# Attention: key transposes from word copies, inside the next key-value block

## The chip, the cores and the metric

The kernel runs on one core of one Trainium2 chip. The metric is the device time of one execution in microseconds, taken as the median of several runs. TensorE (PE) multiplies and transposes, VectorE (DVE), ScalarE (ACT) and GpSimd (POOL) do elementwise work, SyncE (SP) issues the loads of the weights. PEld is TensorE's loading of the stationary operand. POOL can issue DMAs too, on a queue of its own.

## The reference

A trunk of two layers over 256 tokens with a residual width of 2048: a multi-head latent attention, then a Mamba-2 mixer, each followed by a squared-ReLU MLP. All is fp32. The change is in the attention, which has 16 heads and runs once:

```python
q = (rms_norm(c_q, q_norm_g) @ w_uq).reshape(B, S, MLA_HEADS, QK_HEAD_DIM)
kv = (rms_norm(c_kv, kv_norm_g) @ w_ukv).reshape(B, S, MLA_HEADS, QK_NOPE_DIM + V_HEAD_DIM)
k_nope, v = jnp.split(kv, [QK_NOPE_DIM], axis=-1)
k = jnp.concatenate([k_nope, k_rope], axis=-1)       # k_rope: one for all heads
q, k = rms_norm(q, qn_g), rms_norm(k, kn_g)
# rotary embedding of the last 64 of 192 columns of q and k
s = jnp.einsum('bqhd,bkhd->bhqk', q_blk, k) * scale
p = jax.nn.softmax(jnp.where(mask, s, -jnp.inf), axis=-1)
o = jnp.einsum('bhqk,bkhd->bqhd', p, v)
```

## The kernel before

Tokens lie on partitions, in two tiles of 128. Matrix products take each weight as a sum of two parts that TensorE multiplies in a fast rounded format (float32r): ScalarE rounds the loaded weight (`wh`, L102), VectorE computes the rest (`wl`, L103). The main products of a block are L339 and L340 (with `wh`) and L343 (with `wl`).

The attention works in eight **units** of two heads. What has to be multiplied along the head dimension is transposed on TensorE, as a product with the identity; L937 does it on tiles held as float32r, L939 and L985 on fp32 tiles. For the transposes of a **word copy** a DMA that POOL issues copies an fp32 tile, bit by bit, into a tile declared float32r; the queries of units 1 to 7 have such a copy (`qw`, L897).

The loop at L1018 has one **pass** for each u from 0 to 7. Different units are in different steps at a time. In pass u, TensorE's order (which is the order in which the code is written; the order on the other engines is set by a scheduler at build time) is:

- `s0q(u + 1)`: the query block of unit u + 1, two weight units of 384 columns; in pass 7 a block of the output projection (`wob`) stands here.
- `s1(u - 1, "k")`: the six 128x128 transposes of the keys of unit u - 1, the **key group**. Four go into one PSUM bank and two into the next. ScalarE evacuates the first bank (L948), VectorE the second (L946), which holds the rope columns of both heads.
- `s0kv(u)`: the key-value block of unit u, two weight units of 512 columns. Between its two **halves** stands `s3(u - 2)`: the six transposes of the probabilities of unit u - 2 (L985), evacuated by VectorE (L987) and ScalarE (L989). After the block ScalarE takes sums of squares (L296) and POOL computes a root (L289, L290).
- `s2(u - 1)`: the scores of unit u - 1 (L961 and L962, per head), then the softmax on VectorE and ScalarE; its last step is a scaling on VectorE (L975).
- `s4(u - 2)`: probabilities times values (L997, L998).
- `s1(u, "q")`: the six transposes of the queries, the **query group**. With a word copy five come from it (L937) and the last one from the fp32 tile (L939).

Beside these, `k_norm(u)` writes the normalized keys `kn` (VectorE L916, ScalarE L918), `q_norm` the queries (L887), and `q_rope` rotates the queries on POOL (L798 to L801) and issues their word copy. After the loop the keys of unit 7 are transposed, and the last scores and outputs are computed between blocks of the output projection.

The line in `s1` that chooses between the two kinds of transposes takes a word copy wherever one exists, for keys as for queries:

```python
src, words = U[u][name + "n"], U[u].get(name + "w")
...
if words is not None and (i, t) != (1, 1):
```

Of the kernel before, what the change touches and what calls it, by code (L numbers as in the profile page):

```python
# [20 lines left out]
F32 = mybir.dt.float32  # L21
F32R = mybir.dt.float32r
# [6 lines left out]
P = 128  # L29
# [6 lines left out]
HD = 192  # L36
# [178 lines left out]
class Trunk:  # L215
# [610 lines left out]
    def mla_body(self, mp, gain):  # L826
        nc, d = self.nc, self.d
# [39 lines left out]
        U = [dict() for _ in range(UNITS)]  # L867

        def s0q(u, accs=None, mid=None):
            U[u]["q"] = self.block([("uq", u)], cqT, n=384, accs=accs, mid=mid)  # L870

        def q_stats(u):
            accs = U[u]["q"]
            ssq = self.stat(4)
            for t in range(2):
                for h in range(2):
                    self.square_sum(accs[t][:, h * HD:(h + 1) * HD], ssq[:, 2 * t + h:2 * t + h + 1], HD ** -0.5)
            U[u]["qr"] = self.root(ssq, eps4, 4)

        def q_norm(u):  # L880
            accs, r = U[u]["q"], U[u]["qr"]
            qn = mp.tile([P, 2, 2 * HD], F32, tag="qn", name=f"qn{u}", bufs=2)
            for t in range(2):
                for h in range(2):
                    rc = r[:, 2 * t + h:2 * t + h + 1]
                    for o, i, n in ((h * P, 0, P), (256 + h * 64, P, 64)):
                        nc.vector.scalar_tensor_tensor(qn[:, t, o:o + n], accs[t][:, h * HD + i:h * HD + i + n], rc,  # L887
                                                       gq[:, i:i + n], ALU.mult, ALU.mult)
            U[u]["qn"] = qn

        def q_rope(u, ins=None):
            qn = U[u]["qn"]
            with self.tc.issue_after(ins) if ins else nullcontext():
                self.rope(mp, qn[:, :, 256:384].rearrange("p t (h f) -> p t h f", h=2))
                if u:
                    U[u]["qw"] = mp.tile([P, 2, 2 * HD], F32R, tag="qw", name=f"qw{u}", bufs=2)
                    nc.gpsimd.dma_start(U[u]["qw"].bitcast(F32), qn)  # L897

        def s0kv(u, mid=None):
            accs = self.block([("ukv", u)], ckvT, mid=mid)  # L900
            v = mp.tile([P, 2, 2, P], F32, tag="v", name=f"v{u}", bufs=3)
            ssq = self.stat(4)
            for t in range(2):
                for h in range(2):
                    self.square_sum(accs[t][:, h * P:(h + 1) * P], ssq[:, 2 * t + h:2 * t + h + 1], HD ** -0.5)
            for t in range(2):
                nc.scalar.activation(v[:, t].rearrange("p h f -> p (h f)"), accs[t][:, 256:512], AF.Copy)
            U[u]["kv"], U[u]["kr"], U[u]["v"] = accs, self.root(ssq, krss, 4), v

        def k_norm(u):  # L910
            accs, r = U[u]["kv"], U[u]["kr"]
            kn = mp.tile([P, 2, 2 * HD], F32, tag="kn", name=f"kn{u}", bufs=2)
            for t in range(2):
                for h in range(2):
                    rc = r[:, 2 * t + h:2 * t + h + 1]
                    nc.vector.scalar_tensor_tensor(kn[:, t, h * P:(h + 1) * P], accs[t][:, h * P:(h + 1) * P], rc, gk[:, 0:P],  # L916
                                                   ALU.mult, ALU.mult)
                    nc.scalar.activation(kn[:, t, 256 + h * 64:320 + h * 64], kro[:, t], AF.Copy, scale=rc)  # L918
            U[u]["kn"] = kn

        def s1(u, name):


            src, words = U[u][name + "n"], U[u].get(name + "w")
            dst = self.ktile(self.xtp, F32)
            if name == "q":
                nc.gpsimd.memset(dst[64:128, 2], 0.0)
                nc.gpsimd.memset(dst[0:64, 3], 0.0)
            for i in range(2):
                b = self.bank()  # L930
                parts = 2 - i
                for j in range(parts):
                    for t in range(2):
                        o = j * 256 + t * P
                        k = (2 * i + j) * P
                        if words is not None and (i, t) != (1, 1):
                            nc.tensor.transpose(b.bitcast(F32R)[:, o:o + P], words[:, t, k:k + P], self.ident_r)  # L937
                        else:
                            nc.tensor.transpose(b[:, o:o + P], src[:, t, k:k + P], self.ident)  # L939
                v = b[:, :parts * 256].rearrange("p (k n) -> p k n", k=parts)  # L940
                if i and name == "q":
                    for h in range(2):
                        r = slice(64 * h, 64 * h + 64)
                        nc.scalar.activation(dst[r, 2 + h], b[r, 0:256], AF.Copy)
                elif (i == 0) == (name == "q"):
                    nc.vector.tensor_copy(dst[:, 2 * i:2 * i + parts], v)  # L946
                else:
                    nc.scalar.activation(dst[:, 2 * i:2 * i + parts], v, AF.Copy)  # L948
            U[u][name + "T"] = dst
# [29 lines left out]
        def s3(u):  # L979
            p = U[u]["p"]  # L980
            pT = self.ktile(self.xtp, F32).rearrange("p a b -> p (a b)")
            for h in range(2):
                b = self.bank()
                for i in range(3):
                    nc.tensor.transpose(b[:, i * P:(i + 1) * P], p[:, h * 384 + i * P:h * 384 + (i + 1) * P], self.ident)  # L985
                if h == 0:
                    nc.vector.tensor_copy(pT[:, 0:384], b[:, 0:384])  # L987
                else:
                    nc.scalar.activation(pT[:, 384:768], b[:, 0:384], AF.Copy)  # L989
            U[u]["pT"] = pT  # L990

        def s4(u):
            pT, v = U[u]["pT"], U[u]["v"]
            b = self.bank()
            for h in range(2):
                o = h * 256
                nc.tensor.matmul(b[:, o:o + 256], v[:, 0, h], pT[:, h * 384:h * 384 + 256], start=True, stop=False)  # L997
                nc.tensor.matmul(b[:, o + P:o + 256], v[:, 1, h], pT[:, h * 384 + 256:h * 384 + 384], start=False, stop=True)  # L998
            h, lo = oT[u // 2]
            k = (u % 2) * 2  # L1000
            self.split_out(h[:, k:k + 2], lo[:, k:k + 2], b.rearrange("p (k n) -> p k n", k=2))
            U[u].clear()
# [4 lines left out]
        def wob(nb, q, accs=None):  # L1007
            return self.block(wo(nb, [q]), self.from_tiles(oT, 4 * q), accs=accs, first=q == 0, last=q == 3)
# [9 lines left out]
        for u in range(UNITS):  # L1018
            if 0 < u and u + 1 < UNITS:
                s0q(u + 1)  # L1020
                q_stats(u + 1)
            if u == UNITS - 1:
                a0 = wob(0, 0)
            if u >= 1:
                s1(u - 1, "k")
            if 0 < u and u + 1 < UNITS:
                q_norm(u + 1)
            s0kv(u, (lambda: s3(u - 2)) if u >= 2 else None)
            if u + 1 < UNITS:
                q_rope(u + 1, self.pow.ins)  # L1030
            if u == UNITS - 1:
                k_norm(u)
            if u >= 1:
                s2(u - 1)
            if u >= 2:
                s4(u - 2)
            s1(u, "q")
            if u < UNITS - 1:
                k_norm(u)
# [568 lines left out]
```

## Time and profile before

| | us |
|---|---|
| median of 3 runs | 2288.17 |
| lowest and highest | 2285.81, 2288.34 |
| the profiled execution, its own time | 2286.35 |
| its span in the profile | 2284.5 |
| the attention loop from pass 1 to the end of pass 7's key-value block | 76.9 to 176.7 |

Starts of instructions are in us from the start of the span. A row of the chain of waits has a start, a length, an engine, the tile written, a source line and, with an x, how many instructions of a kind follow each other; the chain leads from each instruction to what released it. A row of the order of time has start, length, engine, line, operation, tiles and, in brackets, how long the engine was idle before it and what ended that. TensorE's instructions overlap, so that a row of the order of time is longer than what the instruction adds to the chain. TensorE ran at its full granted clock throughout (1.00 in every stretch shown).

### The profile page before, as it was taken

What the parts mean: (1) busy time and instruction counts of PE and PEld (TensorE: products, weight loads), DVE (VectorE), ACT (ScalarE), POOL (GpSimd) and SP (SyncE); (2) the same over time, 40 slices, a digit from 0 to 9 for tenths busy, and PEclk for the clock granted to TensorE, in tenths of its full rate; (3) what the DMA queues carried; (4) which work ended last, traced back from release to release, by engine and by line L of the source; (5) the groups of instructions that cost most, each with busy time, mean ns of one, the idle gap of its engine ahead of it and who ended that gap; (6) DMA issues with size and microseconds to landing.
All of it is one profiled execution on the core that took longest, in us unless ns stands there. A gap on an engine that the chain in (4) does not pass through costs nothing.

```text
span 2284.5 us, 30768 instructions
## 1 busy us (share of the span) xinstructions
PE 2278.1 (100%) x10929; PEld 1889.6 (83%) x10929; DVE 1915.9 (84%) x2318; ACT 1390.1 (61%) x1947; POOL 275.5 (12%) x315
## 2 busy tenths in 40 slices
PE   9999999999999999999999999999999999999999
PEld 7898888888888888888888888888888888888887
DVE  7786698999898897687899688676989889989985
ACT  7775576566666666564666555545666666666663
POOL 1440000000000000100133213121000000000000
PEclk9999999999999999999999999999999999999999
DMA  8545678888888878667888787767688888888874
GB/s 315 173 153 159 211 230 267 259 255 270 264 255 259 267 232 271 227 208 241 277 280 278 245 275 264 229 222 229 204 265 248 259 270 253 260 275 247 267 232 160
DMA packets 167706, 557.16 MB, mean 244 GB/s; under 512 B 19040, under 2 KB 28192, under 8 KB 166528
## 3 DMA queue, kind: packets, MB, share of 16 engines
q1 hardware_dynamic: 151264, 502.44, 66.2%
q0 software_dynamic: 13888, 48.49, 10.0%
q10 hardware_dynamic: 2400, 4.27, 0.5%
q8 instruction: 86, 1.41, 0.3%
q14 instruction: 68, 0.56, 0.1%
HBM read 529.65 MB, written 6.41 MB: 235 GB/s over the span
## 4 chain that ended last, share of the span: by engine, by line
PE 96%; DVE 1%; DMA 1%; ACT 1%; issue 1%; POOL 0%; SPq 0%; ACTq 0%; DVEq 0%
PE acc L339 13%; PE acc L340 13%; PE acc L343 13%; PE yp L618 9%; PE yp L617 9%; PE yp L616 9%; PE st L617 7%; PE st L618 7%; PE st L616 7%; DMA wraw<-mi 1%; PE sm L324 1%; DVE wl L103 1%; PE y L1309 1%; PE sm L322 1%; PE acc L616 1%; PE acc L618 1%
## 5 line engine op out<-in xcount | busy, mean ns | idle before, releaser
L102 ACT ACTIVATE wh<-wraw 128x1024 fp32r<-128x1024 f32 (+1 forms) x818 | 856.2, 1053 | 570.4 <-PE acc L340 268.9
L103 DVE TENSOR_TENSOR wl<-wraw,wh 128x1024 fp32r<-128x1024 f32 (+1 forms) x818 | 985.5, 1221 | 240.6 <-ACT wh L102 216.6
L616 PE MATMUL yp<-wh,k 128*128 128x512 f32 x896 | 349.2, 390 | 0.0
L618 PE MATMUL yp<-wh,k 128*128 128x512 f32 x896 | 348.8, 389 | 0.0
L617 PE MATMUL yp<-wl,k 128*128 128x512 f32 x896 | 348.6, 389 | 0.0
L339 PE MATMUL acc<-wh,xt 128*128 128x512 f32 x704 | 279.7, 397 | 0.4 <-ACT wh L102 0.4
L340 PE MATMUL acc<-wh,xt 128*128 128x512 f32 x704 | 274.9, 390 | 0.1
L102 ACT ACTIVATE wh<-wrx 128x1024 fp32r<-128x1024 f32 x168 | 177.8, 1058 | 153.4 <-PE yp L618 101.7
L103 DVE TENSOR_TENSOR wl<-wrx,wh 128x1024 fp32r<-128x1024 f32 x168 | 204.3, 1221 | 36.6 <-ACT wh L102 35.6
L618 PEld LDWEIGHTS yp<-wh,k 128*128 128x128 f32 x896 | 168.2, 188 | 35.1
L617 PEld LDWEIGHTS yp<-wl,k 128*128 128x128 f32 x896 | 168.2, 188 | 34.9
L616 PEld LDWEIGHTS yp<-wh,k 128*128 128x128 f32 x896 | 168.2, 188 | 34.8
L339 PE MATMUL acc<-wh,k 128*128 128x512 f32 x496 | 196.5, 396 | 0.0
L340 PE MATMUL acc<-wh,k 128*128 128x512 f32 x496 | 193.3, 390 | 0.0
L343 PE MATMUL acc<-wl,xt 128*128 128x512 f32 x704 | 188.3, 389 | 0.0
L616 PE MATMUL st<-wh,xt 128*128 128x512 f32 x448 | 177.7, 397 | 0.0
L618 PE MATMUL st<-wh,xt 128*128 128x512 f32 x448 | 174.9, 390 | 0.0
L617 PE MATMUL st<-wl,xt 128*128 128x512 f32 x448 | 174.7, 390 | 0.0
L339 PEld LDWEIGHTS acc<-wh,xt 128*128 128x128 f32 x704 | 132.7, 188 | 29.4 <-ACT wh L102 1.6
L340 PEld LDWEIGHTS acc<-wh,xt 128*128 128x128 f32 x704 | 132.5, 188 | 28.5 <-issue 1.2
L343 PEld LDWEIGHTS acc<-wl,xt 128*128 128x128 f32 x704 | 132.1, 188 | 27.7
L199 POOL DMA_DIRECT2D wrx<-mi x56 | 49.2, 878 | 720.6 <-DVE wl L103 524.5
(318 smaller groups left out, 3527.0 us busy)
## 6 DMA issues: line engine op xcount, KB each, us to landing
wraw<-mi SPq DMA_DIRECT2D x256, 512.0 KB, 5.5
wraw<-mo SPq DMA_DIRECT2D x256, 512.0 KB, 5.6
wraw<-si SPq DMA_DIRECT2D x160, 512.0 KB, 5.2
wraw<-so SPq DMA_DIRECT2D x64, 512.0 KB, 5.2
wrx<-mi SPq DMA_DIRECT2D x56, 512.0 KB, 5.4
wrx<-mi POOLq DMA_DIRECT2D x56, 512.0 KB, 7.8
wraw<-wo SPq DMA_DIRECT2D x32, 512.0 KB, 4.0
taps<-xD SPq DMA_DIRECT2D x16, 768.0 KB, 8.4
```

The costliest lines, as they stand in the source:

```text
L102: self.last = nc.scalar.activation(h[:, v], raw[:, v], AF.Copy)
L103: self.last_lo = nc.vector.tensor_tensor(lo[:, v], raw[:, v], h[:, v].bitcast(F32), ALU.subtract)
L199: nc.gpsimd.dma_start(st["b11"].tile, quarter(d, 1, 0), accum_op=ALU.add)
L322: self.nc.tensor.transpose(b.bitcast(F32R)[:, v], words[:, v], self.ident_r)
L324: self.nc.tensor.transpose(b[:, v], src[:, v], self.ident)
L339: nc.tensor.matmul(accs[t][:, :n], ah, wh[:, q, :], start=first and kt + q == 0, stop=False)
L340: nc.tensor.matmul(accs[t][:, :n], al, wh[:, q, :], start=False, stop=False)
L343: nc.tensor.matmul(accs[t][:, :n], lhs(kt + q, t)[0], wl[:, q, :], start=False, stop=en and q == nk - 1)
L616: nc.tensor.matmul(b, ah, wh, start=first and q == 0, stop=False)
L617: nc.tensor.matmul(b, ah, wl, start=False, stop=False)
L618: nc.tensor.matmul(b, al, wh, start=False, stop=last and q == 1)
L1309: nc.tensor.matmul(y[t][c, o], part(t)[:, c], xg[g][t][:, o], start=True, stop=True)
```

## The change

Keys get a word copy as well: at the end of `k_norm` POOL issues a DMA from `kn` into a float32r tile `kw` (two buffers of 3 KB per partition). The key group takes five of its six transposes from it. And two steps change places: the probabilities' transposes `s3(u - 2)` stand where the key group stood, in front of the key-value block, and the key group stands between the block's halves. In pass 1 there are no probabilities yet, so that nothing stands in front of the block.

```diff
@@ -917,6 +917,8 @@
             U[u]["kn"] = kn
+            U[u]["kw"] = mp.tile([P, 2, 2 * HD], F32R, tag="kw", name=f"kw{u}", bufs=2)
+            nc.gpsimd.dma_start(U[u]["kw"].bitcast(F32), kn)
@@ -1021,11 +1023,11 @@
             if u == UNITS - 1:
                 a0 = wob(0, 0)
-            if u >= 1:
-                s1(u - 1, "k")
+            if u >= 2:
+                s3(u - 2)
             if 0 < u and u + 1 < UNITS:
                 q_norm(u + 1)
-            s0kv(u, (lambda: s3(u - 2)) if u >= 2 else None)
+            s0kv(u, (lambda: s1(u - 1, "k")) if u >= 1 else None)
```

Lines behind the first added ones have a number higher by two in the changed file: L937 becomes L939, L939 becomes L941, L946 becomes L948, L985 becomes L987.

TensorE in pass 2, before, from the end of the query block of unit 3 to the first matmul of the second half (`kn1` holds the keys of unit 1, `xt_128` the probabilities of unit 0, `wh29` and `wh30` the two weight units of the key-value block):

```order
L343 MATMUL acc_139_1137<-wl28_1025,cq0_199 128x384
L939 MATMUL yp_148_1188<-ident_97,kn1_1127 128x128 x4
L939 MATMUL sm_149_1194<-ident_97,kn1_1127 128x128 x2
L339 MATMUL acc_150_1207<-wh29_1042,ckv0_201 128x512
...
L343 MATMUL acc_151_1208<-wl29_1043,ckv0_201 128x512
L985 MATMUL yp_153_1228<-ident_97,xt_128_1082 128x128 x3
L985 MATMUL sm_154_1233<-ident_97,xt_128_1082 128x128 x3
L339 MATMUL acc_150_1207<-wh30_1140,ckv0_201 128x512
```

The same place in the changed kernel (`kw1` is the word copy):

```order
L343 MATMUL acc_139_1141<-wl28_1016,cq0_199 128x384
L987 MATMUL yp_148_1192<-ident_97,xt_128_1084 128x128 x3
L987 MATMUL sm_149_1197<-ident_97,xt_128_1084 128x128 x3
L339 MATMUL acc_150_1211<-wh29_1044,ckv0_201 128x512
...
L343 MATMUL acc_151_1212<-wl29_1045,ckv0_201 128x512
L939 MATMUL yp_153_1232<-ident_97,kw1_1138 128x128 x4
L939 MATMUL sm_154_1238<-ident_97,kw1_1138 128x128
L941 MATMUL sm_154_1238<-ident_97,kn1_1129 128x128
L339 MATMUL acc_150_1211<-wh30_1144,ckv0_201 128x512
```

The two groups have changed places around the block's first half, and the key group reads `kw1` for five transposes and `kn1` for one.

POOL between passes 0 and 1, before (`qn1` and `qw1` are the queries of unit 1 and their word copy; the last three rows begin the roots of the query of unit 2 and of the keys of unit 1):

```order
L801 TENSOR_TENSOR qn1_855<-ra_100_918,rb_101_919 128x2x128
L897 DMA qw1_924<-qn1_855 128x768
L289 TENSOR_TENSOR st_112_996<-st_107_987,eps4_462 128x4
L290 TENSOR_TENSOR st_113_997<-st_112_996,mhalf_98 128x4
L289 TENSOR_TENSOR st_124_1070<-st_119_1059,krss_460 128x4
```

and after:

```order
L801 TENSOR_TENSOR qn1_855<-ra_100_918,rb_101_919 128x2x128
L897 DMA qw1_924<-qn1_855 128x768
L921 DMA kw0_949<-kn0_940 128x768
L289 TENSOR_TENSOR st_112_998<-st_107_989,eps4_462 128x4
L290 TENSOR_TENSOR st_113_999<-st_112_998,mhalf_98 128x4
L289 TENSOR_TENSOR st_124_1072<-st_119_1061,krss_460 128x4
```

The key copy of unit 0 stands behind the query copy of unit 1 in POOL's queue. In each later pass it stands behind the query copy of the next unit in the same way, except for unit 7, which has no query copy ahead of it.

VectorE in pass 4 around the query's norm, before (`sm_223` holds the keys of unit 3 transposed, `yp_227` the probabilities of unit 2):

```order
L946 COPY xt_221_1597<-sm_223_1604 128x256
L887 SCALAR_TENSOR_TENSOR qn5_1608<-acc_212_1546,st_220_1594,cst_96 128x128
...
L887 SCALAR_TENSOR_TENSOR qn5_1608<-acc_213_1547,st_220_1594,cst_96 128x64
L987 COPY xt_226_1637<-yp_227_1638 128x384
L103 TENSOR_TENSOR wl41_1651<-wraw41_1548,wh41_1650 128x1024
L103 TENSOR_TENSOR wl42_1756<-wraw42_1566,wh42_1755 128x1024
L965 ISA xt_238_1690,st_239_1691<-yp_243_1695,mk_203 128x128
```

and after:

```order
L989 COPY xt_221_1605<-yp_222_1606 128x384
L887 SCALAR_TENSOR_TENSOR qn5_1616<-acc_212_1554,st_220_1602,cst_96 128x128
...
L887 SCALAR_TENSOR_TENSOR qn5_1616<-acc_213_1555,st_220_1602,cst_96 128x64
L103 TENSOR_TENSOR wl41_1659<-wraw41_1556,wh41_1658 128x1024
L948 COPY xt_226_1645<-sm_228_1652 128x256
L103 TENSOR_TENSOR wl42_1766<-wraw42_1574,wh42_1765 128x1024
L967 ISA xt_238_1698,st_239_1699<-yp_243_1703,mk_203 128x128
```

The evacuation of the keys' rope columns, which stood ahead of the norm, now stands between the two conversions behind it; that of the probabilities took its old place. It is so in passes 3, 4 and 5; in passes 1, 2 and 6 it stands right behind the norm, ahead of both conversions. SyncE's loads are in the same order as before.

## The prediction

> **What bounds the kernel now.** I read the page first, then the busy time of each engine in stretches of the attention loop, then the chain of waits through one pass, then POOL's, VectorE's and SyncE's instructions in order of time.
>
> ```profile
> PE 2278.1 (100%) x10929; PEld 1889.6 (83%) x10929; DVE 1915.9 (84%) x2318; ACT 1390.1 (61%) x1947; POOL 275.5 (12%) x315
> ```
>
> TensorE is busy for 2278.1 of 2284.5 us, so only two things can move the time: TensorE work added or removed, and waits of TensorE. In the rows below (stretch, length, then busy time of PE, PEld, DVE, ACT and POOL, the granted clock, DMA share, GB/s) the stretches are two passes of the loop over head pairs, each cut at the end of a key-value block.
>
> ```profile
> 97.50:113.67 16.17, 15.62 (x92) 14.01 (x92) 13.28 (x40) 11.44 (x40) 7.70 (x11) 1.00 0.45 146
> 113.67:129.10 15.43, 15.43 (x92) 14.03 (x92) 12.55 (x38) 11.46 (x40) 6.85 (x11) 1.00 0.44 147
> ```
>
> The second has no gap on PE: its length is its matmuls. The first is pass 3 and is 16.17 - 15.43 = 0.74 us longer, nearly all of it idle. So the change can win TensorE's own time and that 0.74 us, and it can lose what it makes TensorE wait for.
>
> **Term 1, the cheaper transposes.** The chain through pass 5 shows both kinds: the query's group (five from the word copy, one fp32) and the key's group (six fp32).
>
> ```profile
> 148.47 0.30 PE yp L937 x4
> 148.77 0.08 PE sm L937
> 148.85 0.14 PE sm L939
> ...
> 153.16 0.44 PE yp L939 x4
> 153.59 0.22 PE sm L939 x2
> ```
>
> The query's group takes 0.30 + 0.08 + 0.14 = 0.52 us, the key's 0.44 + 0.22 = 0.66. The changed key group has the form of the query's, so each saves 0.14 us. Units 1 to 7: -0.98 us; unit 0 is in term 2. [...]
>
> **Term 2, the first key copy.** The new copy is a DMA that POOL issues when a unit's keys are normalized. In pass 1 TensorE reaches its use soonest, because no probabilities exist yet that could stand in front of the block. PE's chain there:
>
> ```profile
> 76.22 0.70 PE acc L343 x4
> 76.92 0.69 PE yp L939 x4
> 77.61 0.22 PE sm L939 x2
> 77.82 0.23 PE acc L339
> ...
> 79.67 0.91 PE acc L343 x4
> ...
> 82.39 0.91 PE acc L343 x4
> ```
>
> The query block of unit 2 ends at 76.92. Now the key group follows, and the key-value block's halves take 80.58 - 77.82 = 2.76 and 83.30 - 80.58 = 2.72 us. After the change the first half starts at 76.92 and is done at 79.68; then the transposes want the copy of unit 0. (Its accumulators are free in time: the second is wanted at 77.38, and the norm that reads it, the first row below, ends at 77.22.) When is it there? VectorE, then POOL, in order of time (start, length):
>
> ```profile
> 76.09 1.13 DVE L916 SCALAR_TENSOR_TENSOR kn<-acc,st,cst 128x128 f32<-128x128 f32 x4 [0.59 <-POOL st L290]
> ```
>
> ```profile
> 78.75 0.80 POOL L897 DMA_DIRECT2D qw<-qn  x1 [0.33 <-POOL qn L801]
> ```
>
> The keys are written by 77.22, but in POOL's queue the copy stands behind the query's copy of unit 1, so it is issued at 78.75 + 0.80 = 79.55. How long such a copy (same 384 KB, same queue) takes to land, over all seven and then for the one of pass 1; what SyncE issues beside it, and how long that takes; and the DMA engines, last two numbers of each stretch, share and GB/s:
>
> ```profile
> DMA to landing us min/median/max: 2.6/2.7/4.8
> ...
> DMA to landing us min/median/max: 4.8/4.8/4.8
> ```
>
> ```profile
> 79.26 1.20 SPq L85 DMA_DIRECT2D wraw<-ukv  x2
> ```
>
> ```profile
> L85 SPq DMA_DIRECT2D wraw<-ukv x2: 327/328/328, 79.3 to 80.1; - x2
> DMA to landing us min/median/max: 4.9/5.1/5.3
> ```
>
> ```profile
> 79.00:80.00 1.00, 1.00 (x6) 0.80 (x6) 1.00 (x2) 1.00 (x8) 0.55 (x1) 1.00 0.00 0
> 83.00:84.00 1.00, 1.00 (x8) 0.92 (x7) 1.00 (x3) 1.00 (x6) 0.00 (x0) 1.00 1.00 410
> 84.00:85.00 1.00, 1.00 (x8) 0.94 (x7) 1.00 (x2) 1.00 (x6) 0.41 (x1) 1.00 0.43 168
> ```
>
> The one of pass 1 is the slow one: two weight loads of 512 KB go out 0.5 us behind it, the engines are full to about 84.43, and it lands at 83.55. The key copy adds 0.393 MB to this full stretch: at 410 GB/s 0.96 us, so I let it land at 85.4. TensorE waits 85.4 - 79.68 = 5.7 us, runs the group (0.52) and the second half (2.72), and ends the block at 88.64 instead of 83.30: **+5.34 us**. Low end: nothing shared, 2.6 us after issue, 82.15, block end 85.39, +2.09. High end: behind both loads, 80.1 + 5.3 + 0.96 = 86.4, block end 89.6, +6.3. I take 5.34, because the neighbour in the same queue met these loads and took 4.8. Behind the waiting transposes ScalarE's and VectorE's evacuations of that group queue up, and behind those the next weight conversions; they were converted ahead, and TensorE, which they serve, stands still as well.
>
> [...]
>
> **The copies of the later units** cost nothing as long as two things cover them. In pass 5:
>
> ```profile
> 150.92 0.62 POOL L897 DMA_DIRECT2D qw<-qn  x1
> 156.32 0.19 POOL L289 TENSOR_TENSOR st<-st,eps 128x4 f32<-128x4 f32 x1 [4.78 <-ACT s L296]
> ```
>
> ```profile
> 156.55 0.33 PE yp L985 x3
> ```
>
> The key copy is issued at 151.54; the transposes now stand where L985 stands, at 156.55. That is 5.0 us for a landing of 2.7 in the median and 4.8 at worst. If that cover went, each 0.1 us beyond it would be TensorE's wait. SyncE issues the same loads in the same order. POOL's next instruction (L289) has 4.78 us of idle time ahead of it, more than the 0.62 of the added issue.
>
> **Term 3, the probabilities' transposes, 3.4 us earlier.** They need the softmax's last scaling (L975). Where the key group begins now, the second half of theirs would begin 0.33 us later.
>
> ```profile
> 107.01 0.54 DVE L975 TENSOR_SCALAR xt<-xt,st 128x128 f32<-128x128 f32 x2
> 152.80 0.54 DVE L975 TENSOR_SCALAR xt<-xt,st 128x128 f32<-128x128 f32 x2
> ```
>
> ```profile
> 107.08 0.44 PE L939 MATMUL yp<-ident,kn 128*128 128x128 f32 x2 [0.55 <-ACT xt L944]
> ```
>
> In pass 5: 153.16 + 0.33 = 153.49, and the scaling ends at 153.34, so 0.15 us are left. In pass 3 it ends at 107.55, later than the wait of today ends (107.08): with nothing else moved +0.45 us; with the wait gone -0.74. The softmax there follows a conversion pair that the stall of term 2 lets VectorE finish sooner, so I take -0.32.
>
> **Term 4, the keys' evacuation.** VectorE copies the rope part of the keys (L946) before the query's norm (L887) today, between two conversions (L103) behind it afterwards, in passes 3 to 5. In pass 3, VectorE, then PE's chain (its last row, the first matmul pair of a score, is that of pass 1):
>
> ```profile
> 109.67 0.42 DVE L946 COPY xt<-yp 128x256 f32<-128x256 f32 x1
> 111.44 1.89 DVE L887 SCALAR_TENSOR_TENSOR qn<-acc,st,cst 128x128 f32<-128x128 f32 x8 [1.35 <-POOL st L290]
> ...
> 113.71 2.35 DVE L103 TENSOR_TENSOR wl<-wraw,wh 128x1024 fp32r<-128x1024 f32 x2
> ```
>
> ```profile
> 112.75 0.91 PE acc L343 x4
> ```
>
> ```profile
> 83.30 0.22 PE yp L961 x2
> ```
>
> Norm until 113.33, one conversion (half of 2.35), the copy (0.42, the starts overlapping a little): about 114.85. The block ends at 113.66, and the scores' second matmul wants the copy 0.22 later, at 113.88: up to 0.97 us late. Whatever TensorE waits once, VectorE is ahead in the next pass, so it is paid once, not three times. Ends 0 and 3 x 0.97 = 2.9; I take +0.6, since the earlier terms shift the phase by some 0.3.
>
> **Sum.** 5.34 - 0.98 - 0.32 + 0.60 = **+4.64 us**. Against the profiled execution (2286.35 us, span 2284.5) that is 2290.99. That execution is 1.82 us below the median of the runs; on the median 2288.17 the sum gives **2292.8 us**, +0.20%.
>
> **Rivals.**
> 1. The first key copy lands as fast as an undisturbed one (2.6 us after issue): the median row speaks for it, the 4.8 of its neighbour against. 2.09 - 0.98 - 0.32 + 0.6 = +1.4: 2289.6.
> 2. The late evacuation of term 4 recurs in passes 3, 4 and 5, if VectorE's own round takes as long as TensorE's: for it, VectorE's stretch is busy 12.55 of 15.43 us and chained to ScalarE and POOL. 4.64 - 0.6 + 2.9 = +6.9: 2295.1.
> 3. Not slower: the first key copy is hidden. It decides at a landing by 79.68. Then the block ends at 76.92 + 2.76 + 0.52 + 2.72 = 82.92, -0.38, and the sum is -0.38 - 0.98 - 0.32 + 0.6 = -1.1: 2287.1. Against it: keys written at 77.22 plus 2.6 is already 79.82, and POOL isn't free before 79.55.
> 4. The copies are late in every pass, because weight loads meet them: 5.0 us of cover against a worst landing of 4.8 behind a query copy. At 0.5 us in six passes +3.0 more: 2295.8.
>
> **How the numbers follow.** Forecast 0.54, rival 1 0.15, rival 2 0.15, rival 3 0.08, rival 4 0.08. A difference of 0.2% is 4.6 us, about what a measurement of this kernel can tell from no change; the forecast sits on that edge, its own range (+3.3 to +5.9) being a little more above it than below: 0.32 and 0.22. Slower: 0.32 + 0.15 + 0.08 = 0.55. Within: 0.22 + 0.15 + 0.06 = 0.43. Faster: 0.02, what of rival 3 could be larger than its price. The low end takes in rival 1 and most of rival 3, the high end rivals 2 and 4 with some spread of the runs: 2287.5 to 2297.0.
>
> **What would show it.** In the profile after: the key group at 0.52 us; one PE wait of some 5.7 us in pass 1 at the first transposes of the key's words (L937, in the changed file L939), released by a DMA near 85.4; later key groups without a wait; pass 3 shorter than 16.17; one wait of under 1 us before a scores' second matmul. Wrong it would be if the first copy lands near 82, if the scores wait for the keys' evacuation (L946, then L948) in several passes, or if TensorE waits for a key copy after pass 1.

## The result and the profile after

The changed kernel takes 2294.87 us in the median of six runs (2293.95 to 2295.66). Beside it, the kernel before took 2285.93 us in six runs (2285.26 to 2288.34; the three runs shown above were a part of them). The ratio is 1.0036, with a 95% interval of 1.0023 to 1.0049: the change costs 8.9 us. The profiled execution took 2294.49 us, with a span of 2292.4.

TensorE is busy for 1.0 us more than before, and the span is 7.9 us longer. So most of the loss is idle time. First the page's row of TensorE, then the view of its waits (tile, line, what was waited for; us in total, times, longest):

```profile
PE 2279.1 (99%) x10929; PEld 1889.6 (82%) x10929; DVE 1913.6 (83%) x2318; ACT 1389.9 (61%) x1947; POOL 275.8 (12%) x323
```

```profile
PE yp L939 <- DMA kw<-kn: 6.1, 1, 6.1
...
PE sm L964 <- DVE xt L948: 0.6, 1, 0.6
```

One wait of 6.1 us for a key copy, and no second one. It is the copy of unit 0, in pass 1. POOL issues it behind the query copy; the next rows are POOL's order of time, the landing times of all eight key copies, and the chain of waits from that copy on (start, length, what), with a later key group as the last row:

```profile
78.34 0.80 POOL L897 DMA_DIRECT2D qw<-qn  x1 [0.32 <-POOL qn L801]
79.13 0.57 POOL L921 DMA_DIRECT2D kw<-kn  x1
```

```profile
DMA to landing us min/median/max: 2.6/3.2/6.4
```

```profile
79.13 6.44 DMA kw<-kn
...
85.62 0.75 PE yp L939 x4
86.37 0.13 PE sm L939
86.50 0.23 PE sm L941
86.73 0.43 PE acc L339
...
89.02 0.24 PE acc L339
...
101.29 0.30 PE yp L939 x4
```

The copy needs 6.4 us, twice what the others need. Behind the wait something else shows: the group's first four transposes take 0.75 us, where the same four take 0.30 at 101.29, and a matmul of the block takes 0.43 us until shortly before 89, then 0.24. The granted clock (the third number from the end in rows of stretches) says why:

```profile
81.00:82.00 1.00, 0.00 (x0) 0.00 (x0) 0.93 (x5) 0.00 (x0) 0.04 (x1) 0.88 0.97 395
...
87.00:88.00 1.00, 1.00 (x4) 0.81 (x3) 1.00 (x2) 0.00 (x1) 0.00 (x0) 0.50 0.00 0
88.00:89.00 1.00, 1.00 (x5) 0.79 (x4) 0.32 (x1) 0.00 (x0) 0.00 (x0) 0.71 0.00 0
```

TensorE stopped at 79.5. Its clock fell to half while it stood still: 0.88 over the stretch from 81 to 82 puts the fall at 81.76. It came back at 88.58, by the same reckoning. From 85.62 to 88.58 TensorE worked at half speed. The key group took 0.75 + 0.13 + 0.23 = 1.11 us instead of 0.52, and the second half (86.73 to 90.41) 3.68 instead of 2.72: 1.55 us more, of which half speed over these 2.96 us accounts for 1.48. The block of pass 1 ends at 90.41. Before, it ended at 83.30, and pass 1 began 0.4 us later there: 7.5 us have been lost at this place.

The passes behind it, as stretches from one block's end to the next (pass 3, then pass 4), and the wait that begins the second of them:

```profile
104.57:120.10 15.53, 15.53 (x91) 13.91 (x91) 12.79 (x36) 11.35 (x40) 7.25 (x12) 1.00 0.52 172
120.10:136.35 16.25, 15.61 (x93) 14.07 (x92) 13.32 (x38) 11.76 (x40) 6.80 (x12) 1.00 0.49 162
```

```profile
121.04 0.46 PE L964 MATMUL sm<-xt,xt 128*128 128x128 f32 x2 [0.64 <-DVE xt L948]
```

Pass 3 is 0.64 us shorter than before (16.17), pass 4 0.82 longer (15.43). The wait at the block's end, which was in no pass before, is the scores' second matmul waiting for VectorE's evacuation of the rope columns.

### The profile page after: what moved, and what is told of

It is laid out like the page before. It is cut to its first block, busy times and chain, and to the rows that moved or that the text cites. A ratio compares the mean times of both kernels' runs of the same rounds, so it can differ in the third digit from the quotient of the medians.

```text
span 2292.4 us, 30801 instructions
## 1 busy us (share of the span) xinstructions
PE 2279.1 (99%) x10929; PEld 1889.6 (82%) x10929; DVE 1913.6 (83%) x2318; ACT 1389.9 (61%) x1947; POOL 275.8 (12%) x323
## 4 chain that ended last, share of the span: by engine, by line
PE 96%; DVE 1%; DMA 1%; ACT 0%; issue 0%; POOL 0%; SPq 0%; ACTq 0%; DVEq 0%; POOLq 0%
PE acc L339 13%; PE acc L340 13%; PE acc L343 13%; PE yp L618 9%; PE yp L617 9%; PE yp L616 9%; PE st L617 7%; PE st L618 7%; PE st L616 7%; PE sm L324 1%; PE y L1311 1%; PE sm L322 1%; PE acc L618 1%; PE acc L617 1%; PE acc L616 1%; DVE wl L103 1%
```

## The experiments

Each kernel ran beside the kernel before on the same chip, whose median was 2285.93 to 2286.53 us. "Difference" is against that median. The intervals reach 2 to 3 us to each side, so a single difference below 2 us means little; where several pairs of kernels give the same figure, that is the evidence.

| kernel | median us | difference | ratio, 95% interval |
|---|---|---|---|
| changed kernel | 2294.87 | +8.94 | 1.0023 to 1.0049 |
| 1 unit 0 without a copy | 2288.05 | +1.65 | 1.0000 to 1.0018 |
| 2 the wait filled | 2292.39 | +5.99 | 1.0017 to 1.0036 |
| 3 first copy ahead | 2290.43 | +4.03 | 1.0010 to 1.0028 |
| 4 exchange of places alone | 2288.59 | +2.19 | 1.0000 to 1.0018 |
| 5 copies in the old order | 2295.62 | +9.29 | 1.0026 to 1.0053 |
| 6 like 1, rope columns on ScalarE | 2285.98 | -0.35 | 0.9990 to 1.0008 |
| 7 changed kernel, rope columns on ScalarE | 2293.35 | +6.82 | 1.0018 to 1.0041 |
| 8 like 4, rope columns on ScalarE | 2286.74 | +0.21 | 0.9993 to 1.0011 |
| 9 no query copy ahead | 2289.82 | +3.49 | 1.0004 to 1.0023 |
| 10 late start | 2286.03 | +0.06 | 0.9993 to 1.0011 |

In these kernels the lines behind an edit have numbers up to three higher than in the changed kernel (L939 is L940 in 1 and 6, for example).

**1. Unit 0 without a copy.**

```diff
-            U[u]["kw"] = mp.tile([P, 2, 2 * HD], F32R, tag="kw", name=f"kw{u}", bufs=2)
-            nc.gpsimd.dma_start(U[u]["kw"].bitcast(F32), kn)
+            if u:
+                U[u]["kw"] = mp.tile([P, 2, 2 * HD], F32R, tag="kw", name=f"kw{u}", bufs=2)
+                nc.gpsimd.dma_start(U[u]["kw"].bitcast(F32), kn)
```

> Unit 0 gets no word copy; its key group is six fp32 transposes, all else as in the changed kernel. Theory A (the loss is TensorE's wait for the first copy and the half clock behind it, 7.5 us in pass 1): no wait in pass 1, its block ends 0.2 to 0.4 us earlier than before, the later passes keep their net of about -0.1, and the whole is within 1.5 us of the kernel before (8 to 9 us faster than the changed one). Theory B (the loss sits in the later passes, in late evacuations or in the copies' traffic): still 4 us or more above before.

Measured: +1.65 us (theory A had at most 1.5), no wait for any copy, clock 1.00 throughout. So 7.3 of the 8.9 us are the first copy's. The rest is above 0, though the cheaper groups are all in. TensorE waits for the rope columns again, as in the changed kernel:

```profile
114.97 0.46 PE L965 MATMUL sm<-xt,xt 128*128 128x128 f32 x2 [0.67 <-DVE xt L949]
```

VectorE's order of time there: the copy stands between two conversions, and begins 0.48 us after the scores' first matmul, which starts at 113.92.

```profile
113.27 1.22 DVE L103 TENSOR_TENSOR wl<-wraw,wh 128x1024 fp32r<-128x1024 f32 x1
114.40 0.42 DVE L949 COPY xt<-yp 128x256 f32<-128x256 f32 x1
114.74 1.22 DVE L103 TENSOR_TENSOR wl<-wraw,wh 128x1024 fp32r<-128x1024 f32 x1
```

**2. The wait filled.** 24 products with the identity into the bank that the first key group overwrites, so that TensorE is busy while the copy lands.

```diff
+                if name == "k" and u == 0 and i == 0:
+                    for _ in range(24):
+                        nc.tensor.matmul(b, self.ident_r, ckv[0].rearrange("p a b -> p (a b)")[:, :512], start=True, stop=True)
```

> The changed kernel, with 24 products of the identity with a finished tile in front of the first key group, which the transposes overwrite; they fill 5.5 us of the 6.1 us wait, and the wait for the copy stays. Clock theory (the matmuls behind the wait are slow because the granted clock falls to 0.50 after about 2.3 us of idle TensorE): the clock stays at 1.00, the group takes 0.52 and the second half 2.72 us, and the whole is 1.5 us below the changed kernel, some 7.4 above before. Rival (they are slow because the copy and the weight loads disturb SBUF or PSUM): group and half as slow as in the changed kernel, +8.9 above before.

Measured: +5.99 us, 2.95 below the changed kernel, where 1.5 was expected. TensorE's order of time:

```profile
79.56 5.78 PE L936 MATMUL yp<-ckv,ident 128*128 128x512 f32 x24
85.69 0.54 PE L942 MATMUL yp<-ident,kw 128*128 128x128 f32 x4 [0.35 <-DMA kw<-kn]
...
88.12 1.07 PE L343 MATMUL acc<-wl,ckv 128*128 128x512 f32 x4
```

The copy lands as late as before (6.3 us after its issue). The clock stays at 1.00, and the block ends at 88.12 + 1.07 = 89.2 instead of 90.41. So the half clock follows from TensorE's standing still and is a cost of its own. Its size differs between the profiles (1.2 us at this place) and the medians (2.95); experiment 7 shows a possible reason.

**3. The first copy ahead.** The keys of unit 0 are normalized and copied before POOL rotates the queries of unit 1, so that the copy meets neither the query copy nor the weight loads.

```diff
-            nc.gpsimd.dma_start(U[u]["kw"].bitcast(F32), kn)
+            self.copied = nc.gpsimd.dma_start(U[u]["kw"].bitcast(F32), kn)
...
             s0kv(u, (lambda: s1(u - 1, "k")) if u >= 1 else None)
+            if u == 0:
+                k_norm(u)
             if u + 1 < UNITS:
-                q_rope(u + 1, self.pow.ins)
+                q_rope(u + 1, (self.pow if u else self.copied).ins)
...
-            if u < UNITS - 1:
+            if 0 < u < UNITS - 1:
                 k_norm(u)
```

> The changed kernel with the first key copy issued by POOL ahead of the rotation and copy of unit 1's queries, when the keys are written (76.9) instead of at 79.1. Queue theory: it lands before the weight loads get going, 2.6 to 3.2 us after its issue, at 79.5 to 80.1; TensorE waits 0.2 to 0.8 us at full clock, and the whole is -0.5 to +1.5 us against before. Rival (the first copy is slow wherever it is issued, since it is among the first DMAs of POOL's queue): it lands at 82 or later, and the whole is +4 or more.

Measured: +4.03 us, outside the queue theory's range. The number is the rival's (+4 or more), its mechanism is not: the copy is not slow here and does what it was meant to. Issued at 77.63, it is there for TensorE at 80.48, and TensorE waits 0.82. But the rotation now stands behind it. POOL's root for the query of unit 2 comes at 83.11 instead of the 79.71 of the changed kernel, VectorE's query norm waits for that root, and the rope columns stand behind the norm. POOL, VectorE and TensorE in order of time:

```profile
77.63 0.80 POOL L921 DMA_DIRECT2D kw<-kn  x1 [1.81 <-ACT xt L946]
...
83.11 0.21 POOL L289 TENSOR_TENSOR st<-st,eps 128x4 f32<-128x4 f32 x1
```

```profile
84.46 1.89 DVE L887 SCALAR_TENSOR_TENSOR qn<-acc,st,cst 128x128 f32<-128x128 f32 x8 [2.88 <-POOL st L290]
86.27 0.41 DVE L948 COPY xt<-sm 128x256 f32<-128x256 f32 x1
```

```profile
86.74 0.49 PE L964 MATMUL yp<-xt,xt 128*128 128x128 f32 x2 [2.53 <-DVE xt L948]
```

A new wait of 2.53 us took the old one's place, and the clock fell behind it too (0.50 from 87.16 to 90.56).

**4. The exchange of places alone**, with no key copy at all.

```diff
-            U[u]["kw"] = mp.tile([P, 2, 2 * HD], F32R, tag="kw", name=f"kw{u}", bufs=2)
-            nc.gpsimd.dma_start(U[u]["kw"].bitcast(F32), kn)
```

> No word copies of keys at all, only the exchange of the two transposes' places. Theory A: pass 1 ends 0.2 to 0.4 us earlier, pass 3 loses its idle time (-0.5), passes 4 and 6 wait for the keys' evacuation (0.6 and 0.3), no group gets cheaper: -0.5 to +1 us against before. Theory B (the exchange itself costs, through late evacuations or probabilities that aren't ready): +3 us or more.

Measured: +2.19 us, between the two expectations. The copies of units 1 to 7 (experiment 1 against this one) are worth 0.54 us by these medians, where the prediction has 0.98, a difference within the noise; and the exchange of places costs something by itself.

**5. Copies in the old order**, for units 1 to 7 (the edit is against the kernel of experiment 1).

```diff
-            if u >= 2:
-                s3(u - 2)
+            if u >= 1:
+                s1(u - 1, "k")
...
-            s0kv(u, (lambda: s1(u - 1, "k")) if u >= 1 else None)
+            s0kv(u, (lambda: s3(u - 2)) if u >= 2 else None)
```

> Copies for units 1 to 7, but the places as before: the key group ahead of the key-value block, the probabilities' transposes inside it. (Unit 0 has no copy, so the first wait is out of it.) Theory A (the exchange of places is what hides the later copies): in pass 5 of the kernel before the key group begins at 153.16, and a key copy issued at 151.54 that takes the 3.2 us of the kernel after lands at 154.7, so TensorE waits about 1.6 us in each of passes 2 to 7, about 9 us in all, less 0.14 x 7 = 1.0 for the cheaper groups: +8 against before, 2294 us; if the clock doesn't fall in waits this short, it reads 1.0 throughout. Rival (a wait is paid once, and POOL and VectorE are ahead afterwards, so that the next copy is issued earlier): one wait of 1.6 to 3 us, later ones under 0.3 us, +1 to +3, 2287 to 2289.

Measured: +9.29 us, near theory A's +8. TensorE waits for the copy in five passes: 3.69 us in pass 2 and 0.94 in each of the next four, of which the first and the last:

```profile
94.63 0.72 PE L940 MATMUL yp<-ident,kw 128*128 128x128 f32 x4 [3.69 <-DMA kw<-kn]
113.82 0.51 PE L940 MATMUL sm<-ident,kw 128*128 128x128 f32 x4 [0.94 <-DMA kw<-kn]
...
163.12 0.51 PE L940 MATMUL yp<-ident,kw 128*128 128x128 f32 x4 [0.94 <-DMA kw<-kn]
```

So the cover of later copies is what the exchange of places buys, and a late copy is not paid once but in five passes. Behind the wait of 3.69 us the clock is at 0.50 until 100.80; behind the four short ones it never falls.

**6. Rope columns on ScalarE**, in the kernel of experiment 1.

```diff
-                elif (i == 0) == (name == "q"):
+                elif i == 0 and name == "q":
                     nc.vector.tensor_copy(dst[:, 2 * i:2 * i + parts], v)
```

> The kernel without the first key copy, and both evacuations of a key group (the 128 columns and the rope columns) on ScalarE instead of ScalarE and VectorE. If the waits of the scores for the rope columns (0.7 and 0.2 us there) are what keeps that kernel at +1.65 us, they go, and it comes out 0.7 to 1.0 us lower, at +0.6 to +1.0 against before, without a wait of a scores' matmul for a copy by VectorE. Rival (another late evacuation, now ScalarE's, or VectorE's lead shows up elsewhere): +1.6 or more, and the waits of TensorE are as long in sum, on other rows.

Measured: -0.35 us, below both expectations: 2.0 below experiment 1, more than the 0.9 us of listed waits that went. The loop shows where. The stretches run from the middle of one pass's block to that of the next: the four from pass 2 to pass 6 in experiment 1, then the first two of them in this kernel.

```profile
95.25:110.82 15.57, 15.57 (x93) 14.01 (x91) 12.45 (x36) 11.83 (x40) 7.62 (x13) 1.00 0.54 174
110.82:127.00 16.18, 15.51 (x93) 13.98 (x91) 12.88 (x38) 11.92 (x40) 7.44 (x13) 1.00 0.56 185
127.00:142.31 15.31, 15.31 (x94) 13.93 (x91) 12.17 (x35) 11.67 (x40) 6.35 (x12) 1.00 0.54 177
142.31:157.97 15.66, 15.54 (x94) 14.01 (x91) 13.16 (x36) 12.09 (x40) 6.34 (x13) 1.00 0.54 183
```

```profile
94.96:110.25 15.29, 15.29 (x93) 13.90 (x91) 12.12 (x35) 12.15 (x41) 7.32 (x13) 1.00 0.54 178
110.25:125.56 15.31, 15.31 (x94) 13.93 (x91) 12.11 (x35) 12.18 (x41) 6.93 (x13) 1.00 0.57 181
```

With the columns on ScalarE each round takes 15.3 us: the 15.43 of pass 4 before, less 0.14 for the cheaper group. With them on VectorE three of the four are 0.3 to 0.9 us longer.

**7 and 8. The same edit in the changed kernel, and in the exchange of places alone.** The diff is that of experiment 6.

> The changed kernel with one edit: both evacuations of a key group on ScalarE. Theory (the late evacuation of the rope columns by VectorE is a second loss beside the first copy, and the two add up): the edit took 2.1 us off the kernel without the first copy, so it takes 1.5 to 2.5 us off the changed kernel, 2292.4 to 2293.4, at +6.0 to +7.0 against before; the wait for the first copy stays at about 6.1 us with the clock at 0.50 behind it, and no scores' matmul waits for VectorE. Rival (the stall in pass 1 already puts VectorE ahead, so nothing is left to gain but the one wait of 0.6 us): 2294 to 2295, +7.7 to +8.5.

> The exchange of places alone, without any key copy (the key groups are six fp32 transposes), and both evacuations of a key group on ScalarE. Against the kernel that has the copies of units 1 to 7 and the same evacuations (-0.35 us against before) it tells what the cheaper groups are worth by themselves. Theory (0.14 us in each of seven units): 0.98 us slower than that kernel, +0.6 against before, 2287.0. Rival (the gain is lost in waits elsewhere): level with it, 2286.0. [...]

Measured: +6.82 us, as the theory of 7 had it, and +0.21 us, which lies between the theory of 8 (+0.6) and its rival (level with experiment 6, -0.35). In 7 no scores' matmul waits any more, and the wait for the first copy is the old one. But its clock fell later: 0.69 in the stretch from 84 to 85 and 0.89 in that from 91 to 92 put the half clock at 84.38 to 91.22.

```profile
84.00:85.00 1.00, 0.00 (x0) 0.00 (x0) 0.47 (x1) 0.00 (x0) 0.00 (x0) 0.69 0.99 406
...
91.00:92.00 1.00, 1.00 (x8) 0.89 (x7) 0.25 (x1) 0.78 (x5) 0.00 (x0) 0.89 0.00 0
```

TensorE resumes at 85.69 here, so 5.5 us of work ran at half speed, which is 2.8 us lost, where the changed kernel's profiled execution lost 1.5 behind the same wait. So the price of nearly the same stall differs between these two executions: in one the clock fell 2.26 us after TensorE had stopped (79.50 to 81.76), in the other 4.54 us (79.84 to 84.38), and it then stayed at half for nearly the same time, 6.82 and 6.84 us. Why it fell at these times was not shown. If the time differs between executions of one kernel too, which was not measured, that can account for the 2.95 of experiment 2.

With these, the parts can be read off the traces too: from the last four matmuls of the query block in pass 1 to those of an output projection's block behind the loop, start to start, in the kernel before (it begins at 76.22, a row shown above), 8, 6 and 1:

```profile
208.28 0.91 PE acc L343 x4
```

```profile
76.45 0.70 PE acc L343 x4
...
208.62 0.91 PE acc L343 x4
```

```profile
76.09 0.70 PE acc L343 x4
...
207.48 0.91 PE acc L343 x4
```

```profile
76.09 0.70 PE acc L343 x4
...
209.26 0.91 PE acc L343 x4
```

That is 132.06, 132.17, 131.39 and 133.17 us: the exchange +0.11, the copies -0.78, the rope columns on VectorE +1.78.

| part | by medians | by this stretch |
|---|---|---|
| exchange of places (8 against before) | +0.2 | +0.11 |
| word copies of units 1 to 7 (6 against 8; 1 against 4) | -0.56; -0.54 | -0.78 |
| rope columns stay on VectorE (1 against 6; changed against 7; 4 against 8) | +2.0; +2.1; +2.0 | +1.78 |
| first key copy (changed against 1; 7 against 6) | +7.3; +7.2 | |

The four add up to 0.2 - 0.55 + 2.0 + 7.25 = 8.9 us, the whole of the result. By one path through the kernels (before, 8, 6, 1, changed) they must. What is evidence is that three pairs of six different kernels give the rope columns the same 2.0 to 2.1 us; the agreement of the pairs in the second and the fourth row follows from that. The kernel before was not run with the columns on ScalarE. Its passes 4 to 6 take 15.44 us without a wait, where those of 8 take 15.42, so that there is nothing to win there.

**9. No query copy ahead.** The queries of unit 1 are transposed as fp32, and the first key copy takes their copy's place in the queue.

```diff
-                if u:
+                if u > 1:
                     U[u]["qw"] = mp.tile([P, 2, 2 * HD], F32R, tag="qw", name=f"qw{u}", bufs=2)
```

> The query group of unit 1 is made of fp32 throughout and its word copy is left out, so that the first key copy stands alone in POOL's queue; the two weight loads stay. Theory A (the first landing is late because the copy stands behind another copy and meets the weight loads): it is issued at about 78.4 instead of 79.1 and lands at 82.5 to 83.2 (as the query copy of pass 1 did before: 4.2 to 4.8 us), so TensorE waits 3.0 to 3.9 us instead of 6.1, and the clock still falls, since the wait is longer than the 2.3 us after which it fell: 2 to 3 us below the kernel after, +6 to +7 against before, 2292 to 2293. Rival (the loads alone set the landing): it lands at 85.3 to 85.6 as it does now, the wait is 5.8 to 6.1 us and the time that of the kernel after, +9.

Measured: +3.49 us, further in the first theory's direction than it said (+6 to +7), and outside both ranges. The chain, and the stretches in which the clock fell and came back:

```profile
78.11 3.18 DMA kw<-kn
...
81.33 0.54 PE yp L939 x4
```

```profile
82.00:83.00 1.00, 1.00 (x5) 0.81 (x5) 1.00 (x6) 0.50 (x1) 0.00 (x0) 0.68 0.93 299
...
85.00:86.00 1.00, 1.00 (x4) 0.81 (x3) 0.00 (x0) 0.80 (x1) 0.00 (x0) 0.61 0.41 49
```

The copy lands within 3.2 us, as the later ones do. It is issued 0.9 us ahead of the weight loads (79.01) and lands at 81.29, 2.3 us behind the issue of the first of them. The copy of the changed kernel is issued at 79.13, 0.3 us behind the first of them (78.87). The query copies of the changed kernel and of the kernel before go out 0.5 us ahead of the loads and land after 4.2 and 4.8 us. So the landing of these four copies goes with the place of the issue before or behind these loads; whether the query copy's own bytes add to it was not taken apart. And the clock fell after a wait of only 1.70 us, when TensorE was already working again.

**10. Late start.** In 6, 8 and 1 the exchange of places gave less than the wait of 0.74 us in pass 3 that it removes. The trace of experiment 6 shows another wait in pass 2, where the first probabilities' transposes are. The chain there leads back to a table load on ScalarE, ahead of the softmax's first exponential; TensorE's two groups of three both come late. From the end of the query block (89.61 + 0.86 = 90.47) to the key-value block's first matmul (92.19 in the chain) it takes 1.7 us, where the six transposes alone take 0.66:

```profile
87.75 1.28 ACT L974 ACT_TABLE_LOAD   x1
```

```profile
90.61 0.70 PE L988 MATMUL yp<-ident,xt 128*128 128x128 f32 x3
91.49 0.70 PE L988 MATMUL sm<-ident,xt 128*128 128x128 f32 x3 [0.18 <-DVE xt L978]
```

So in this kernel copies and exchange begin with unit 2 and pass 3; the rope columns are on ScalarE (the edit is against experiment 6).

```diff
-            if u:
+            if u > 1:
                 U[u]["kw"] = mp.tile([P, 2, 2 * HD], F32R, tag="kw", name=f"kw{u}", bufs=2)
...
-            if u >= 2:
+            if u > 2:
                 s3(u - 2)
+            elif u:
+                s1(u - 1, "k")
...
-            s0kv(u, (lambda: s1(u - 1, "k")) if u >= 1 else None)
+            s0kv(u, (lambda: s1(u - 1, "k")) if u > 2 else (lambda: s3(u - 2)) if u == 2 else None)
```

> The kernel with both key evacuations on ScalarE, but passes 1 and 2 keep the order of the kernel before and units 0 and 1 have no key copy; copies and the exchange of places begin with unit 2 and pass 3. Theory (in pass 2 the first softmax, behind a table load of 1.28 us on ScalarE, is too late for the probabilities' transposes in their earlier place, which there take 1.88 us instead of 0.66): the 1.2 us of pass 2 are not lost, six cheaper groups save 0.84, so 2284.9, 1.0 to 1.5 us below before, and pass 2 is 14.2 us long. Rival (that delay was also what let pass 3's softmax come in time): pass 2 is 14.2 us, but the probabilities' transposes of pass 3 wait 0.5 to 1.0 us, and the time is 2285.5 to 2286.5, level with before.

Measured: +0.06 us; the rival was right. The wait has moved to pass 3:

```profile
106.96 0.61 PE L988 MATMUL yp<-ident,xt 128*128 128x128 f32 x3 [0.97 <-DVE xt L978]
```

In both places where the probabilities' transposes were first moved, the softmax is not ready for them, and TensorE waits about a microsecond once. The chain to this wait has no table load (it goes through the exponentials on ScalarE, L974 at 104.73, to VectorE's scaling, which ends at 106.82), so that the load is not what makes this wait, though one lies on the chain in pass 2. No version was found that is measurably faster than the kernel before.

## Why the prediction was right or wrong

The forecast (2292.8 us, slower by 4.64) had the direction and the main cause; the median, 2294.87, lies inside the range. That is in part luck: the range was laid around 2288.17, the median of three runs, where six runs give 2285.93. Laid around that, it would have ended at 2294.8, just below the measured time. The size of the change was about half of the 8.9 us measured; term 2 is short by 1.9 us and term 4 by 1.4. Rival 2's 2295.1 came nearest in number, but it stands on the same high median, and half clock is not in it. Step by step:

**Term 1, the cheaper groups (-0.98).** The durations were right: a key group with words takes 0.52 us, and passes without a wait take 15.3 us against 15.43. Against the kernel without copies 0.55 us arrived in the medians, 0.78 in the traced stretch, which has six of the seven groups (0.84).

**Term 2, the first key copy (+5.34).** This is the step that failed most in size, by 2 us. The mechanism was right: issued behind the query copy, met by the two weight loads, one wait of TensorE, at the place named. Landing was taken as 85.4 and came at 85.58, but TensorE reached its transposes 0.2 us sooner, so that the wait was 6.1 instead of 5.7. What the sum did not have at all is the clock: a standing TensorE was priced at its idle time, and the work behind it at full speed. At half clock that work took 1.55 us more in the profiled execution. With the wait 0.4 us longer and a first half of 3.00 instead of 2.76 us (76.50 to 79.50) that is the 2.2 us between 5.34 and the 7.5 by which the block's end moved. The runs give 7.2 to 7.3 for this copy.

The trace of before had no place where this could be read, since its clock is 1.00 in all stretches of the loop. Behind the waits it reads 0.50 for 6.82 us after the change and for 3.42 us in experiment 9, where a wait of 1.70 us was enough.

**The later copies (0).** Right: they land 3.2 us after issue and nothing waits for them. Experiment 5 shows what the cover is worth: without it 0.94 us in each of four passes, and 3.69 with a half clock behind it in another. Rivals 1, 3 and 4 are out.

**Term 3, the probabilities' transposes earlier (-0.32).** Pass 3 became 0.64 us shorter, 0.14 of it by term 1, so the gain there was undersized: 0.50 us (and in experiment 7, without the delays told under term 4, pass 3 takes only 15.31). But the term looked at passes 3 and 5 only. In pass 2, where the softmax comes first, the same move costs about 1 us in every kernel without the stall; in the changed kernel the stall in pass 1 covers nearly all of it (pass 2 takes 14.16 us, before 14.20).

**Term 4, the keys' evacuation (+0.6, once).** The wait came at the scores' second matmul, released by L948, and was 0.64 us. That it is paid once was wrong. Moving the columns to ScalarE takes about 2.0 us off, in three pairs of kernels, and the stretches of experiment 1 show the loss in three of four rounds. This is rival 2's mechanism, and nearer to its 2.9 than to the 0.6. The list of waits shows only the one of 0.64 us in the changed kernel, but its rounds show more. Cut where the scores' first matmul starts, these are the rounds of passes 4 and 6 in the changed kernel, then that of pass 4 in experiment 7:

```profile
120.02:136.19 16.17, 15.53 (x91) 13.99 (x90) 13.40 (x38) 11.68 (x40) 6.80 (x12) 1.00 0.49 163
...
151.50:167.12 15.62, 15.51 (x91) 13.97 (x90) 12.88 (x38) 12.10 (x40) 6.75 (x12) 1.00 0.58 187
```

```profile
120.86:136.17 15.31, 15.31 (x92) 13.93 (x91) 12.53 (x36) 11.96 (x41) 6.49 (x12) 1.00 0.55 173
```

All four rounds from pass 3 to 6 take 15.3 us in experiment 7. In the changed kernel those of passes 3, 4 and 6 take 0.31, 0.86 and 0.31 us longer, and that of pass 5 the same. Set beside experiment 7, the whole delay arises at the scores' second matmul in passes 4 and 6; in pass 3 about half does, and half at the probabilities' transposes. That is 1.5 of the 2.1 us of the medians.

What stays open: what share of the first landing is the query copy's and what the loads', how the loss to the clock is spread over executions of one kernel, and why the softmax comes late where the probabilities' transposes are first moved.

## What to carry to other kernels

A wait of TensorE cost more than its length here (the waits of 1.70 us and more did, those of 0.94 did not): look for what the clock does behind a new wait. A step that is moved forward in a pipeline of passes has to be checked in the first pass in which it is moved too: here the stage that feeds it was not ready there. And when a copy is put on a queue, look which loads go out just ahead of it: with 1.2 us of difference in their order, and one more copy ahead in its queue, the landing went here from 3.2 to 6.4 us.

## What the runs showed of the hardware

The granted clock, worked out from stretches as above (a mean of 0.68 over a stretch that ends in 0.50 puts the fall at 0.36 of it):

| kernel | TensorE idle | half clock | length |
|---|---|---|---|
| 9 | 79.63 to 81.33 (1.70) | 82.36 to 85.78 | 3.42 |
| 3 | 84.21 to 86.74 (2.53) | 87.16 to 90.56 | 3.40 |
| 5, pass 2 | 90.94 to 94.63 (3.69) | 93.96 to 100.80 | 6.84 |
| 7 | 79.84 to 85.69 (5.85) | 84.38 to 91.22 | 6.84 |
| changed | 79.50 to 85.62 (6.12) | 81.76 to 88.58 | 6.82 |
| 5, passes 3 to 6 | four times 0.94 | none | |

The lengths were 3.42 and 3.40 us behind the two shorter of these waits (1.70 and 2.53 us) and 6.82 to 6.84 behind the three longer ones (3.69 to 6.12 us). The fall came 2.3 to 4.5 us after the idling began, in 9 and 3 when the work had already resumed. The wait of 1.70 us thus cost another 1.7 us behind it (3.42 us at half speed).

The delay of the fall does not follow the length of the wait: 2.73 us in 9, 2.95 in 3, 3.02 in 5, 4.54 in 7 and 2.26 in the changed kernel. What sets it was not shown. Between the wait of 0.97 us in 10, whose clock has a mean of 1.000 over the span, and the one of 1.70 in 9 the loop had none in these traces, so that they do not show from what length on a wait brings the clock down.
